# Second-part rows of a channel mixer split ahead of the first part's last down products, and its first two up tiles read from them

## The chip, the core and the metric

The kernel runs on one core of one Trainium2 chip. The time is device microseconds of one execution. Three runs of the kernel before are shown below; the profile and the trace are of a fourth execution of its own.

## What is computed

One inference step of a two-layer decoder trunk over 512 prompt rows and 32 sample rows, 1024 features wide. The reference, cut to what matters here:

```python
def swiglu(x, wg, wu, wd):
    return (jax.nn.silu(x @ wg) * (x @ wu)) @ wd          # D_FF = 2816
...
x = x + 0.5 * swiglu(rmsnorm(x, norm_ffa[i]), ffa_wg[i], ffa_wu[i], ffa_wd[i])
h = rmsnorm(x, norm_mix[i])
out = rwkv7_time_mix(h, ...) if i % 2 == 0 else mlstm_mix(h, ...)
x = x + out
x = x + 0.5 * swiglu(rmsnorm(x, norm_ffb[i]), ffb_wg[i], ffb_wu[i], ffb_wd[i])
```

The change is at the first channel mixer (`f0a`) and at the start of the RWKV mixer of layer 0.

## The kernel before

The 544 rows are held with features on the partitions, as eight tiles `x[k]` of 128x544, and are cut into two parts: rows 0 to 255 (`PARTS[0]`, 256 columns) and rows 256 to 543 (`PARTS[1]`, 288 columns). Every product is made of three TensorE instructions (`mm3`, L404 to L408) on operands split into a high and a low half; a weight tile of 128x1024 is loaded into one of three `wr` buffers, and each 512-wide half of it is rounded by ScalarE into `wh` (L401) and its remainder made by VectorE into `wl` (L402). There are four `wh` and four `wl` buffers, which is two weight tiles.

First `ffn` runs the whole mixer `f0a` for the first part: `norm_split` allots eight tiles `ts` of 128x2x544 (tag `a2`, ten buffers) and fills the high and low halves of `x * gain` into the columns of the first part alone (`split_scaled`, L454 on ScalarE and L455 on VectorE); the columns of the second part stay unused. Then come 22 up tiles (a `_g` and a `_u` product each, 24 matmuls a product) and eight down tiles (66 matmuls each, L493), each ending in an update of `x[m]` (L496). These use the pool `ffn` and eight PSUM banks `ps`.

Then the pools of `ffn` are closed and `rwkv` begins. The second part's rows of the same mixer are cut into units by `ffn_units` and used as filler between the steps of the RWKV mixer of the first part. `start` allots sixteen tiles `rk` in the new pool, fills them with the split rows, and takes the squares and the factor of the norm, `1/sqrt(mean(x^2)+eps)`, by one matmul pair with ones (L437), an Ln and an Exp. `up(m)` makes the `_g` and `_u` products into the two PSUM banks `pd`, multiplies both by the factor (L540, L541) and makes the sigmoid by Exp, Ln and Exp on ScalarE with three GpSimd operations in between; the result is split into `hm`. `down` adds to `x`. A list `todo` holds the units; `self.step(n)` issues the next n; `FILL` says how many after each step of `first`. The order of issue before is:

```python
self.rwkv_setup()                       # constants; ends with keep_table
first, second = self.rwkv_first(0)      # first[0] is rwkv_norm(0), first[1] mixes rows for w1, ...
self.todo = self.ffn_units(*before, 1, (0, 4, 8, 12, 16, 19, FT))
self.step()                             # start
for q, f in enumerate(first):
    f()
    self.step(FILL.get(q, 0))           # FILL[0] = 4: up0, up1, up2, up3 after rwkv_norm
```

`rwkv_norm(0)` (L697) takes the squares and the factor of the first part's new rows (again a matmul pair L437 into `pd`), multiplies the rows by it (L709) and forms the differences of neighbouring rows (L728, L730). `rwkv_mix` then makes from them the operands `mx` (L744 to L746) of the RWKV projections.

The instructions are not run in that order as it stands: when the kernel is built, a scheduler sets a fixed order for each engine. Of the instructions that are ready it takes the one issued first, so the order of issue is an order of rank; an instruction whose operands and buffers are ready early may be placed long ahead of its place in the program. On the chip each engine then keeps its fixed order and waits on semaphores.

Of the kernel before, what the change touches and what calls it, by code (L numbers as in the profile page):

```python
# [17 lines left out]
P = 128  # L18
D = 1024
KT = 8  # L20
FT = 22
# [5 lines left out]
HA = TP // 2  # L27
HB = TT - HA
# [7 lines left out]
NX = 4  # L36
WW = 512
NW = 4
FILL = {0: 4, 1: 4, 2: 1, 3: 4, 5: 3, 14: 3}
FILL2 = {5: 3, 6: 3, 9: 4}  # L40
PARTS = (slice(0, HA), slice(HA, TT))
NPAIR = 8
# [247 lines left out]
class Trunk:  # L290
# [149 lines left out]
    def norm_split(self, g, parts=PARTS):  # L440

        ts = [self.a2(F32R) for _ in range(KT)]
        rs = [self.tile("rms", 2, [P, HB])[:, :hs.stop - hs.start] for hs in parts]
        for hs in parts:
            self.split_scaled(g, hs, [(t[:, 0, hs], t[:, 1, hs]) for t in ts])
        for i, hs in enumerate(parts):
            for k in range(KT):
                self.squares(k, hs, rs[i])
        return [(t[:, 0, :], t[:, 1, :]) for t in ts], rs
# [7 lines left out]
    def ffn(self, name, g, parts=PARTS):  # L457
        xs, rs = self.norm_split(g, parts)
        hs_ = []
        lo_, hi_ = parts[0].start, parts[-1].stop  # L460
        parts = [(hs, slice(hs.start - lo_, hs.stop - lo_), hs.stop - hs.start) for hs in parts]
        for m in range(FT):
            wg = self.weight(self.a[name + "_g"][m])
            wu = self.weight(self.a[name + "_u"][m])
            hh, hl = [self.local("h", 44, [P, TT], F32R)[:, :hi_ - lo_] for _ in range(2)]
            for i, (hs, ds, w_) in enumerate(parts):
                pg, pu = self.ps(), self.ps()
                for ps, wt in ((pg, wg), (pu, wu)):
                    for k in range(KT):
                        c = slice(k * P, (k + 1) * P)  # L470
                        self.mm3(ps[:, :w_], *wt(c), xs[k][0][:, hs], xs[k][1][:, hs], k == 0, k == KT - 1)
                if m == 0:
                    self.norm_factor(rs[i], self.ps())
                s, w = self.t1(w_), self.t1(w_)
                self.V.tensor_tensor(s, pg[:, :w_], rs[i], op=ALU.mult)
                self.V.tensor_tensor(w, pu[:, :w_], rs[i], op=ALU.mult)
                self.last = self.S.activation(s, s, AF.Silu)
                self.G.tensor_tensor(s, s, w, op=ALU.mult)  # L478
                self.split(hh[:, ds], hl[:, ds], s)
            hs_.append((hh, hl))  # L480
            if m == 1 and name == "f0a":
                self.load_x(1)
        kb = (0, 8, 16, FT)
        for m in range(KT):
            pss = [self.ps() for _ in parts]

            def rows(b):
                return self.weight(self.a[name + "_d"][m][:, kb[b] * P:kb[b + 1] * P])

            def part(b, i, w):  # L490
                hs, ds, w_ = parts[i]
                for k in range(kb[b], kb[b + 1]):
                    c = slice((k - kb[b]) * P, (k - kb[b] + 1) * P)  # L493
                    self.mm3(pss[i][:, :w_], *w(c), hs_[k][0][:, ds], hs_[k][1][:, ds], k == 0, k == FT - 1)
                if b == 2:
                    self.V.scalar_tensor_tensor(self.x[m][:, hs], pss[i][:, :w_], 0.5, self.x[m][:, hs], op0=ALU.mult, op1=ALU.add)  # L496
            if m < KT - 1:
                for b in range(3):
                    w = rows(b)
                    for i in range(len(parts)):  # L500
                        part(b, i, w)
            else:
                ws = [rows(b) for b in range(3)]
                for i in range(len(parts)):
                    for b in range(3):
                        part(b, i, ws[b])
# [4 lines left out]
    def ffn_units(self, name, g, i, groups=(0, 6, 11, 17, FT)):  # L511


        V, S, G = self.V, self.S, self.G
        hs = PARTS[i]
        w_ = hs.stop - hs.start
        xs = []
        rs = self.tile("rms", 2, [P, HB])[:, :w_]
        h = {}

        def start():
            for k in range(KT):
                early = i == 0 and k < NX
                xs.append([self.local("xs", 2 * NX, [P, HA], F32R) if early else self.rk(i, F32R) for _ in range(2)])
            self.split_scaled(g, hs, xs)
            for k in range(KT):
                self.squares(k, hs, rs)
            self.norm_factor(rs, self.bank("pd", 2), True)

        def up(m):  # L530
            ps = []

            def half(n):
                ps.append(self.bank("pd", 2)[:, :w_])
                self.part_dense(self.weight(self.a[name + n][m]), ps[-1], xs)

            def second():
                half("_u")
                s, w, e = self.t1(w_), self.t1(w_), self.t1(w_)
                V.tensor_tensor(s, ps[0], rs, op=ALU.mult)  # L540
                V.tensor_tensor(w, ps[1], rs, op=ALU.mult)  # L541
                self.sigmoid(e, s)
                G.tensor_tensor(s, s, w, op=ALU.mult)
                G.tensor_tensor(s, s, e, op=ALU.mult)
                h[m] = [self.hm(w_) for _ in range(2)]
                self.split(*h[m], s)
            return Unit((24, lambda: half("_g")), (24, second))

        def down(m, k0, k1):
            wt = self.weight(self.a[name + "_d"][m][:, k0 * P:k1 * P])  # L550
            ps = self.bank("pd", 2)
            self.part_dense(wt, ps[:, :w_], [h[k] for k in range(k0, k1)])
            V.scalar_tensor_tensor(self.x[m][:, hs], ps[:, :w_], 0.5, self.x[m][:, hs], op0=ALU.mult, op1=ALU.add)
        us = [start]
        for k0, k1 in zip(groups, groups[1:]):
            us += [up(m) for m in range(k0, k1)]
            us += [Unit((3 * (k1 - k0), lambda m=m, k0=k0, k1=k1: down(m, k0, k1))) for m in range(KT)]
        return us

    def dense_units(self, ap, xs, evac):  # L560
# [47 lines left out]
    def rwkv(self, before=None, after=None):  # L608


        with self.scope("rw", nps=1):
# [4 lines left out]
            with self.tc.tile_pool(name="spill", bufs=1, space=DRAM) as dp:  # L616
# [5 lines left out]
                self.nhm = {"mx": NMX, "hm": 8}  # L622
                self.low, self.lowp = {}, dp
                with self.scope("rw1", nps=0):
                    self.rwkv_setup()
                    first, second = self.rwkv_first(0)
                    self.todo = self.ffn_units(*before, 1, (0, 4, 8, 12, 16, 19, FT))
                    self.step()
                    for q, f in enumerate(first):
                        f()  # L630
                        self.step(FILL.get(q, 0))
                    with self.tc.high_priority(OFF):
                        self.all_of(self.rwkv_ahead(0))
                        self.begin("quad", self.rwkv_square(0))
                        self.all_of(self.rwkv_rows(0))
                        self.drain("quad")
                    for q, f in enumerate(second):
                        f()
                        self.step(FILL2.get(q, 0))
                    with self.tc.high_priority(OFF):  # L640
                        self.all_of(self.rwkv_value(0))
                        self.all_of(self.rwkv_ahead(1))
                    first, second = self.rwkv_first(1)
                    self.todo += first
                    self.rwkv_slots(0, 10)
                    self.todo += second + self.rwkv_out(0, 0, 4)
                    self.rwkv_slots(10, 17)
# [24 lines left out]
    def rwkv_setup(self):  # L672
# [15 lines left out]
        w = self.a2(F32R).rearrange("p a b -> p (a b)")  # L688
        self.hg3 = w[:96, :TT]
        self.lg = w[:, TT:TT + 2 * P], w[:, TT + 2 * P:TT + 3 * P]  # L690
        self.pre = None
        self.keep_table()

    def rk(self, i, dt=F32):
        return self.rp(f"rk{i}", 17, [P, PARTS[i].stop - PARTS[i].start], dt)
# [1068 lines left out]
```

## Time and profile before

| | us |
|---|---|
| runs before | 2484.68, 2488.0, 2490.43; median 2488.0 |
| profiled execution | 2485.8 |
| its span, first to last instruction | 2483.9 |
| mean granted TensorE clock, share of full | 0.98 |

The profiled execution is 1.9 us longer than its span. Times in the rows below are microseconds from the start of the span. PE is TensorE's matmuls, PEld its weight loads, DVE VectorE, ACT ScalarE, POOL GpSimd. In the groups, `x8` is the number of instructions, and behind the bar stand their busy time in us, the mean of one in ns, and the idle time of the engine just before them. In the timelines the idle time ahead of an instruction and what ended it stand in brackets. A clock of 1.00 is the level of 2.4 GHz and 0.50 that of 1.2 GHz; values in between are means over a stretch.

### The profile page before, as it was taken

How to read it: one execution, taken by the hardware profiler on the slowest of the kernel's cores; microseconds unless marked ns; L12 is line 12 of the kernel's file. 1: busy time of each engine (PE TensorE's matmuls, PEld its weight loads, DVE VectorE, ACT ScalarE, POOL GpSimd, SP SyncE). 2: the span in 40 equal slices, each digit the busy share in tenths (PEclk: the TensorE clock that was granted, in tenths of full speed). 3: DMA queues.
4: the chain of work that ended last, by engine and by line, in shares of the span. 5: the costliest groups of instructions: out<-in, count | busy, mean ns of one | idle time of the engine just before them, and what ended most of it. 6: DMA issues, size and time to landing. Idle time of an engine off the chain costs nothing.

```text
span 2483.9 us, 54258 instructions
## 1 busy us (share of the span) xinstructions
PE 2404.3 (97%) x21731; PEld 2291.6 (92%) x21731; DVE 1562.1 (63%) x3202; ACT 1253.5 (50%) x2732; POOL 442.4 (18%) x458
## 2 busy tenths in 40 slices
PE   9998999998899999999999999999999999999997
PEld 8998988987788888898999999999978999999997
DVE  6667787788767888766666544443438766444333
ACT  6555666556676656565555433332345545333322
POOL 1202222333121244321110011110000000111100
PEclk9999999999899999999999999999999999999998
DMA  7564766434464343544555432322323323222232
GB/s 220 186 192 140 233 207 192 125 114 121 134 201 154 118 128 93 151 144 134 162 169 159 123 93 88 92 82 86 90 84 112 86 83 98 86 86 86 90 89 71
DMA packets 118348, 316.81 MB, mean 128 GB/s; under 512 B 14360, under 2 KB 30136, under 8 KB 118096
## 3 DMA queue, kind: packets, MB, share of 16 engines
q1 hardware_dynamic: 118096, 313.35, 41.3%
q8 instruction: 170, 2.79, 0.5%
q14 instruction: 82, 0.67, 0.1%
HBM read 291.34 MB, written 21.96 MB: 126 GB/s over the span
## 4 chain that ended last, share of the span: by engine, by line
PE 60%; DVE 2%; ACT 1%; DMA 1%; issue 0%; SPq 0%; DVEq 0%; POOL 0%; ACTq 0%
PE ps L406 15%; PE ps L408 15%; PE ps L407 15%; PE pd L406 3%; PE pd L407 3%; PE pd L408 2%; PE pc L284 1%; PE ps L284 1%; PE ps L1420 1%; PE ps L1422 1%; PE ps L1421 1%; DMA d<-dc 1%; PE b L284 0%; PE ps L281 0%; DVE wl L402 0%
## 5 line engine op out<-in xcount | busy, mean ns | idle before, releaser
L402 DVE TENSOR_TENSOR wl<-wr,wh 128x512 fp32r<-128x512 f32 (+2 forms) x993 | 692.6, 700 | 450.5 <-ACT wh L401 422.7
L401 ACT CAST wh<-wr 128x512 fp32r<-128x512 f32 (+2 forms) x993 | 593.3, 602 | 625.4 <-PE ps L407 431.6
L406 PE MATMUL ps<-a,wh 128*128 128x288 f32 (+1 forms) x2384 | 697.4, 293 | 13.2 <-DVE raw L1516 5.3
L408 PE MATMUL ps<-a,wl 128*128 128x288 f32 (+1 forms) x2384 | 692.4, 290 | 0.0
L407 PE MATMUL ps<-a,wh 128*128 128x288 f32 (+1 forms) x2384 | 686.7, 288 | 0.3
L406 PEld LDWEIGHTS ps<-a,wh 128*128 128x128 f32 x2384 | 452.6, 190 | 16.2 <-ACT a L454 5.5
L407 PEld LDWEIGHTS ps<-a,wh 128*128 128x128 f32 x2384 | 452.2, 190 | 1.6 <-DVE a L455 1.1
L408 PEld LDWEIGHTS ps<-a,wl 128*128 128x128 f32 x2384 | 449.9, 189 | 0.5 <-DVE wl L402 0.2
L406 PE MATMUL ps<-h,wh 128*128 128x288 f32 (+1 forms) x1056 | 303.9, 288 | 0.0
L407 PE MATMUL ps<-h,wh 128*128 128x288 f32 (+1 forms) x1056 | 303.4, 287 | 0.0
L408 PE MATMUL ps<-h,wl 128*128 128x288 f32 (+1 forms) x1056 | 303.2, 287 | 0.0
L478 POOL TENSOR_TENSOR t<-t,t 128x256 f32<-128x256 f32 (+1 forms) x132 | 141.7, 1074 | 856.7 <-ACT wh L401 409.5
L406 PE MATMUL pd<-rk,wh 128*128 128x288 f32 (+1 forms) x656 | 197.1, 301 | 6.2 <-ACT mx L745 3.7
L408 PEld LDWEIGHTS ps<-h,wl 128*128 128x128 f32 x1056 | 198.9, 188 | 0.0
L407 PEld LDWEIGHTS ps<-h,wh 128*128 128x128 f32 x1056 | 198.9, 188 | 0.0
L406 PEld LDWEIGHTS ps<-h,wh 128*128 128x128 f32 x1056 | 198.6, 188 | 0.0
L407 PE MATMUL pd<-rk,wh 128*128 128x288 f32 (+1 forms) x656 | 194.9, 297 | 0.0
L408 PE MATMUL pd<-rk,wl 128*128 128x288 f32 (+1 forms) x656 | 193.0, 294 | 0.0
L401 ACT CAST h<-t 128x256 fp32r<-128x256 f32 (+1 forms) x132 | 55.3, 419 | 199.2 <-POOL t L478 199.2
L406 PE MATMUL pd<-mx,wh 128*128 128x256 f32 (+1 forms) x448 | 133.1, 300 | 3.3 <-ACT mx L745 2.1
L406 PEld LDWEIGHTS pd<-rk,wh 128*128 128x128 f32 x656 | 125.7, 192 | 10.8 <-ACT mx L745 3.9
L407 PE MATMUL pd<-mx,wh 128*128 128x256 f32 (+1 forms) x448 | 132.9, 298 | 2.7 <-DVE mx L746 2.5
(516 smaller groups left out, 4537.5 us busy)
## 6 DMA issues: line engine op xcount, KB each, us to landing
wr<-in_f0a_u_dram SPq DMA_DIRECT2D x44, 512.0 KB, 3.9
wr<-in_f0b_g_dram SPq DMA_DIRECT2D x44, 512.0 KB, 3.6
wr<-in_f0b_u_dram SPq DMA_DIRECT2D x44, 512.0 KB, 3.6
wr<-in_f0a_g_dram SPq DMA_DIRECT2D x43, 512.0 KB, 3.6
wr<-in_f1a_g_dram SPq DMA_DIRECT2D x22, 512.0 KB, 4.2
wr<-in_f1a_u_dram SPq DMA_DIRECT2D x22, 512.0 KB, 3.5
wr<-in_f1b_g_dram SPq DMA_DIRECT2D x22, 512.0 KB, 3.5
wr<-in_f1b_u_dram SPq DMA_DIRECT2D x22, 512.0 KB, 3.5
```

What stands on the lines that cost most here:

```text
L284: r = f(*a, **k)
L401: self.S.copy(dst_h, src)
L402: self.V.tensor_tensor(dst_l, src, dst_h, op=ALU.subtract)
L406: T.matmul(out, wh, xh, start=start, stop=False)
L407: T.matmul(out, wh, xl, start=False, stop=False)
L408: T.matmul(out, wl, xh, start=False, stop=stop)
L478: self.G.tensor_tensor(s, s, w, op=ALU.mult)
L1420: T.matmul(pss[q][:n, :], xs[k][0][:, ts], wt(cs)[0], start=k == 0, stop=False)
L1421: T.matmul(pss[q][:n, :], xs[k][0][:, ts], wt(cs)[1], start=False, stop=False)
L1422: T.matmul(pss[q][:n, :], xs[k][1][:, ts], wt(cs)[0], start=False, stop=k == KT - 1)
```

## The change

- In `ffn`, for `f0a` and ahead of its third down tile (m = 2), the rows of the second part are split into the unused columns of `ts`, their squares are taken, and their factor is made into a tile `rs1`, by a Sqrt and a VectorE reciprocal in place of Ln and Exp.
- `ffn_units` for the second part uses `rs1`. Its first two up tiles read the split rows from `ts` and not from `rk`. `start` splits the rows into `rk` as before, but without squares and factor, and is now issued third, behind up0 and up1.
- In `rwkv`, up0, up1 and `start` are issued ahead of `rwkv_setup` and `rwkv_norm`; up2 and up3 follow behind `rwkv_norm` (FILL[0] is 2 in place of 4). `keep_table`, which loads ScalarE's table for Ln and Exp, moves from the end of `rwkv_setup` to ahead of up0.

```diff
-FILL = {0: 4, 1: 4, 2: 1, 3: 4, 5: 3, 14: 3}
+FILL = {0: 2, 1: 4, 2: 1, 3: 4, 5: 3, 14: 3}
...
     def norm_split(self, g, parts=PARTS):
         ts = [self.a2(F32R) for _ in range(KT)]
+        self.ts = ts
...
         for m in range(KT):
+            if name == "f0a" and m == 2:
+                self.rs1 = self.tile("rms", 2, [P, HB])
+                self.split_scaled(g, PARTS[1], [(t[:, 0, HA:], t[:, 1, HA:]) for t in self.ts])
+                for k in range(KT):
+                    self.squares(k, PARTS[1], self.rs1)
+                self.norm_factor(self.rs1, self.ps())
             pss = [self.ps() for _ in parts]
...
-        rs = self.tile("rms", 2, [P, HB])[:, :w_]
+        ready = [(t[:, 0, hs], t[:, 1, hs]) for t in self.ts] if i else None
+        rs = self.rs1 if i else self.tile("rms", 2, [P, HB])[:, :w_]
...
             self.split_scaled(g, hs, xs)
-            for k in range(KT):
-                self.squares(k, hs, rs)
-            self.norm_factor(rs, self.bank("pd", 2), True)
+            if not i:
+                for k in range(KT):
+                    self.squares(k, hs, rs)
+                self.norm_factor(rs, self.bank("pd", 2), True)
...
-                self.part_dense(self.weight(self.a[name + n][m]), ps[-1], xs)
+                self.part_dense(self.weight(self.a[name + n][m]), ps[-1], ready if ready and m < 2 else xs)
...
+        if ready:
+            us[:3] = us[1], us[2], us[0]
...
                 with self.scope("rw1", nps=0):
+                    self.todo = self.ffn_units(*before, 1, (0, 4, 8, 12, 16, 19, FT))
+                    self.keep_table()
+                    self.step(3)
                     self.rwkv_setup()
                     first, second = self.rwkv_first(0)
-                    self.todo = self.ffn_units(*before, 1, (0, 4, 8, 12, 16, 19, FT))
-                    self.step()
...
-        self.pre = None
-        self.keep_table()
```

## Rows read from the trace of the kernel before

**Rows 1.** The page's first line: span and number of instructions.

```profile
span 2483.9 us, 54258 instructions
```

**Rows 2.** Stretches: length, each engine's busy time (instructions), clock, DMA share, GB/s.

```profile
140.00:199.50 59.50, 59.50 (x507) 59.40 (x505) 35.66 (x66) 30.83 (x58) 0.00 (x0) 1.00 0.69 199
199.50:203.60 4.10, 1.19 (x5) 0.60 (x5) 3.42 (x11) 4.08 (x10) 0.00 (x0) 1.00 0.88 280
203.60:207.00 3.40, 3.40 (x16) 3.37 (x15) 3.36 (x10) 3.17 (x10) 0.00 (x0) 0.54 0.83 293
...
211.80:215.50 3.70, 0.04 (x1) 0.00 (x0) 3.70 (x13) 2.02 (x6) 0.00 (x0) 0.82 0.15 19
215.50:221.00 5.50, 5.42 (x23) 5.45 (x24) 5.29 (x11) 2.55 (x8) 4.33 (x3) 0.50 0.51 178
221.00:239.90 18.90, 18.90 (x141) 18.51 (x140) 16.45 (x33) 12.38 (x27) 8.12 (x8) 1.00 0.41 119
...
242.30:247.10 4.80, 4.51 (x30) 4.08 (x31) 3.67 (x7) 1.76 (x3) 0.00 (x0) 1.00 0.10 19
...
350.00:353.40 3.40, 0.85 (x8) 0.65 (x7) 3.40 (x7) 2.25 (x4) 1.56 (x2) 1.00 0.44 165
353.40:358.00 4.60, 4.27 (x33) 3.93 (x33) 4.60 (x6) 1.42 (x3) 3.73 (x3) 0.63 0.20 61
```

**Rows 3.** TensorE's timeline from the last down product to the first low-rank product: start, us, instruction, idle before.

```profile
199.32 0.28 PE L408 MATMUL ps<-h,wl 128*128 128x256 f32 x1
201.25 0.75 PE L437 MATMUL pd<-rms,c_c_all 128*128 128x288 f32 x2 [1.65 <-DVE x L496]
203.27 0.70 PE L437 MATMUL pd<-rms,c_c_all 128*128 128x256 f32 x2 [1.26 <-DVE rms L424]
203.62 0.55 PE L406 MATMUL pd<-rk,wh 128*128 128x288 f32 x1
...
215.58 0.58 PE L406 MATMUL pd<-rk,wh 128*128 128x288 f32 x1 [3.74 <-ACT mx L745]
...
242.27 0.53 PE L406 MATMUL pd<-hm,wh 128*128 128x288 f32 x2 [2.35 <-ACT hm L401]
...
247.13 0.28 PE L406 MATMUL pd<-mx,wh 128*128 128x256 f32 x1
```

**Rows 4.** VectorE's timeline at the same place, cut.

```profile
205.41 2.85 DVE L709 SCALAR_TENSOR_TENSOR x<-x,c_vecs,rms 128x256 f32<-128x256 f32 x7
...
212.60 1.28 DVE L402 TENSOR_TENSOR wl<-wr,wh 128x512 fp32r<-128x512 f32 x2
...
214.99 0.45 DVE L540 TENSOR_TENSOR t<-pd,rms 128x288 f32<-128x288 f32 x1
```

**Rows 5.** Groups of VectorE and ScalarE, 199.5 to 242.3 us.

```profile
L454 ACT ACTIVATE rk<-x,c_vecs 128x288 fp32r<-128x288 f32 x8 | 4.0, 525 | 0.0
L455 DVE SCALAR_TENSOR_TENSOR rk<-x,c_vecs,rk 128x288 fp32r<-128x288 f32 x8 | 3.8, 510 | 0.0
L709 DVE SCALAR_TENSOR_TENSOR x<-x,c_vecs,rms 128x256 f32<-128x256 f32 x8 | 3.3, 478 | 0.0
L728 DVE TENSOR_TENSOR gm<-x 128x255 f32<-128x255 f32 x8 | 3.2, 410 | 0.0
```

**Rows 6.** Timelines and a group: what the moved norm factor is made of.

```profile
135.54 1.28 ACT L829 ACT_TABLE_LOAD   x1
17.71 1.75 DVE L433 RECIPROCAL rms<-rms 128x256 f32<-128x256 f32 x1 [1.44 <-ACT rms L432]
L422 ACT ACTIVATE t<-x 128x288 f32<-128x288 f32 (+1 forms) x13 | 5.5, 432 | 2.5 <-DVE x L496 2.3 <-DVE h L402 0.2
```

**Rows 7.** Timelines of VectorE and GpSimd: one operation alone and beside GpSimd.

```profile
227.16 0.47 DVE L744 SCALAR_TENSOR_TENSOR m<-gm,c_vecs,x 128x256 f32<-128x256 f32 x1
228.16 1.03 DVE L744 SCALAR_TENSOR_TENSOR m<-gm,c_vecs,x 128x256 f32<-128x256 f32 x1
...
227.75 1.17 POOL L543 TENSOR_TENSOR t<-t,t 128x288 f32<-128x288 f32 x1
```

## The prediction

> **What bounds the kernel now.** I read four views. The page gives the span [rows 1], and the profiled execution took 2485.8 us, 1.9 us more. The table of stretches then says where TensorE isn't at work or isn't at full clock around the change [rows 2]: through the down products of the first part (140 to 199.5 us) it is busy 59.50 of 59.50 us at clock 1.00, so nothing else limits it there. Then, at the seam to the RWKV mixer, it is busy 1.19 of 4.10 us, works 3.4 us at clock 0.54, stands still for 3.7 us, and works 5.42 us at clock 0.50. From 221 us on it is full again at 1.00. TensorE's timeline names the waits [rows 3]: 1.65 us behind the last update of x, 1.26 us for the squares of the first part's new rows, 3.74 us ahead of up1, and 2.35 us ahead of the first down products that need up3. VectorE's timeline shows what TensorE waited for at 215.58 [rows 4]. The row names ScalarE, but the bank of up0's first product comes free by L540, which starts at 214.99, so that is what ended the wait. L540 stood behind the norm of the first part (L709), the last of the row splits, the weight splits of 212.60 and more: VectorE is busy 3.70 of 3.70 us there. The seam is thus bound by VectorE's queue and by the order of rank in it, and each idle stretch of 3 to 4 us was followed by the lower clock level of 1.2 GHz.
>
> **The change part by part.**
>
> *Work taken ahead of the seam.* Eight splits on ScalarE at 0.525 us and eight on VectorE at 0.510 [rows 5] are added, 4.2 and 4.1 us, since `start` still makes its own. Their operands are there early and they use no pool that opens late, so the scheduler may place them anywhere in the idle time of `f0a`. In the down stretch alone VectorE has 59.50 - 35.66 = 23.8 us free and ScalarE 28.7 [rows 2]. The squares ran among the down products before, too (they are part of the group of L422) [rows 6]. A table load of 1.28 us for Sqrt comes on ScalarE, and a reciprocal on VectorE: 1.75 us for 256 columns, so about 2.0 for 288 [rows 6]. I cost all of this at nothing. What hides it is that two weight tiles are kept ready, four halves, each lasting TensorE about 1.4 us (12 of 507 matmuls of 59.50 us [rows 2]). An operation of 2 us in front of a weight split fits in there; if that cover is gone, the bound is the reciprocal and the table load, 3.3 us. What isn't hidden is the matmul pair of the norm factor, which now stands between down products on a full TensorE: at most the 0.75 us that it took at the seam [rows 3], at least half of that at full clock; I take 0.5.
>
> *Start of up0.* It needs neither the pair nor the splits of `start` any more, but still a bank of the new pool, which before was had only behind L496, at 201.25 [rows 3]. So up0 starts there and not at 203.62: 2.37 us gained (none if another wait stays; 4.0 if the bank comes at once).
>
> *Clock after the seam.* The idle time in front falls to 1.65 us, with a full stream behind it. The nearest row is the wait of 2.35 us ahead of 242.27, after which the clock stayed at 1.00 [rows 2, 3]. So 3.40 us at 0.54 no longer cost 3.40 x 0.46 = 1.6 us (none gained, if it falls all the same).
>
> *Wait of up1.* up0 and up1 now rank above `start` and `rwkv_norm`, so L540 no longer stands behind L709: 3.74 us gained, and the half clock behind it, 5.42 x 0.50 = 2.7 us [rows 2, 3]. Together the seam gives 2.4 + 1.6 + 3.7 + 2.7 = 10.4 us.
>
> *What is late next.* `rwkv_norm`. Its matmul pair needs one of two `pd` banks, and up0 and up1 hold both by rank. Before, it ran at 203.27; now it comes behind up1. Four products at 24 x 18.90/141 = 3.2 us [rows 2] from 201.25 + 0.5 end at 214.6. There the pair costs 0.4 and the handing over of a bank about as much, 0.75 us in all (0.4 to 1.1). up2 runs from 215.3 to 221.7; its splits `rk`, 3.8 us of VectorE [rows 5], have all of up0 and up1 to be made in. L709 started 2.1 us after the pair before (203.27 to 205.41) [rows 3, 4], so now at 216.7, and with L709 and the differences, 3.3 and 3.2 us plus eight one-column operations, VectorE is taken up for some 6.9 us to 223.6 [rows 5]. These rank above up2's L540, which frees the bank of up3, and above up3's weight splits. With an L540 of 0.45 and half a weight tile (0.64) behind them [rows 4], less what overlaps, up3 begins at 224.3 in place of 221.7: a new wait of 2.6 us. It lies between 0, if the scheduler finds room for the splits in between, and 5.8 us, if GpSimd's operations for up1 slow these operations (L744 took 1.03 us beside L543, and 0.47 alone [rows 7]; three GpSimd operations of 1.17 us for an up tile would add 1.9) and a whole weight tile comes behind.
>
> On this the Trainium skill, page "SBUF — State Buffer", section "Who interferes with whom", has a rule that speaks against the change: a VectorE instruction with two SBUF inputs and a GpSimd instruction that reads SBUF exclude each other for the whole of one. The two L744 rows agree [rows 7]. By it the norm, which met no GpSimd work before, now meets that of up1, which puts the wait near 4.6 us and the gain near 2; by the undisturbed rows it is 2.6 and 4.8.
>
> *Clock after the new wait.* 2.35 us of idling was followed by 1.00, but 2.55 us of it (in 350 to 353.4) by 4.60 us at 0.63, 1.7 us lost [rows 2, 3]. 2.6 us is nearer to the second: I take 1.7 (0 to 2.7).
>
> *What stays.* The wait ahead of the first down products is the time of up3's chain through ScalarE and GpSimd less what TensorE has in hand, both unchanged: 2.35 us again. Behind it TensorE is nearly full, so what is gained by then should reach the end.
>
> Sum: 10.4 - 0.5 - 0.75 - 2.6 - 1.7 = 4.85, say 4.8 us. Against the profiled execution that is 2485.8 - 4.8 = 2481.0; the median of the runs is 2.2 higher, so 2488.0 - 4.8 = 2483.2 us.
>
> **The rivals.**
>
> *VectorE keeps up.* No new wait at up3 and no clock loss there: 10.4 - 1.25 = 9.15 us, 2478.9. For it: in 221 to 239.9 VectorE has 2.4 us free [rows 2]. Against it: none of its work has left the seam except the order of it, and 203.6 to 221 was without a gap.
>
> *The wait only moves.* The upper bounds hold, 5.8 us at up3 and 2.7 for the clock: 10.4 - 1.25 - 8.5 = 0.65 us gained, 2487.4; the same if a later stretch that is bound by VectorE, as 350 to 358 (busy 8.00 of 8.00 us [rows 2]), takes the gain back. For it: the L744 rows, and the rule named above, which is a case of this one. Against it: TensorE's lead is carried by all that runs behind it.
>
> *Slower: the norm of the first part comes too late.* If its pair gets a bank only behind up3, at about 227.5, then L709, the differences and eight mixes (0.47 us each alone, 1.03 beside GpSimd [rows 7], and 0.47 for the low half) fill VectorE for 14 to 19 us, and with six weight halves at 0.64 between them the first low-rank product waits until 247 to 250, where it began before at 247.1 [rows 3]. TensorE has the eight products and four down tiles by 237 and idles some 10 us, then starts at half clock (2.7 us); the second mix, queued behind, is later by the same. That is 2 to 9 us lost, around 2494. It decides from the point where the pair slips by more than about 20 us against 203.27. Against it: the pair ranks above up2, so a bank that up1 gives back should go to it.
>
> **How the numbers follow.** A measurement of this kernel can tell about 0.2%, 5.0 us, from no change. Forecast (a shorter wait at up3, gain 2.5 to 8.5 us; own range 2479.5 to 2485.5): 0.58, with a little under half above 5.0 us. VectorE keeps up: 0.16. The wait only moves, or the gain is given back (gain -2 to 2.5): 0.17. Slower: 0.09. So faster is 0.27 + 0.16 = 0.43, within 0.2% 0.31 + 0.17 = 0.48, slower 0.09. The range reaches down to a full gain with the bank had at once (2488.0 - 9.15 - 1.65 = 2477.2) and up to the far end of the third case, 2490.0; the slower case and a strip of the best are left out.
>
> **What would show it.** Right, if the profile of the changed kernel shows: up0's first matmul on tile `a` in place of `rk` at about 201.8 behind L496; a clock of 1.00 from there to about 214, with no wait over 1 us; both 96 matmuls and then the 256-column pair L437; the next wait of 2 to 6 us at up2 or up3 with L709 or L728 in front of L540 on VectorE; and the matmul of 242.27 at about 237.5. The down products stay gapless from 140 to 199.5 but for the pair. Wrong, if the 256-column pair still runs ahead of up0, if splits stand in front of weight splits during `f0a` and TensorE waits there, if the half clock still follows the seam, or if the lead at 237.5 is gone further on.

## The result and the profile after

The changed kernel took 2503.35 us (median of 4 runs, 2501.36 to 2504.78), beside 2488.6 us for the kernel before on the same chip: a ratio of 1.0059, 95% interval 1.0046 to 1.0071. It is slower by 14.7 us; forecast were 2483.2 us and a range from 2477.2 to 2490.0. Measured once more on another chip it took 2502.75 us beside 2491.15, 1.0048 (1.0036 to 1.0060).

The page's first line after, against [rows 1]:

```profile
span 2501.5 us, 54280 instructions
```

The table of stretches after, with the columns of [rows 2]:

```profile
140.00:200.00 60.00, 60.00 (x510) 59.89 (x509) 36.90 (x63) 32.90 (x58) 1.28 (x1) 1.00 0.67 196
200.00:218.20 18.20, 17.16 (x133) 16.77 (x131) 13.36 (x29) 12.01 (x25) 2.90 (x3) 1.00 0.69 211
218.20:226.30 8.10, 0.03 (x2) 0.01 (x1) 4.97 (x11) 4.61 (x12) 2.66 (x3) 0.82 0.36 99
226.30:229.50 3.20, 3.20 (x12) 3.02 (x13) 0.99 (x3) 1.16 (x4) 0.00 (x0) 0.50 0.00 0
229.50:235.00 5.50, 5.50 (x40) 5.41 (x39) 5.50 (x21) 2.83 (x10) 0.00 (x0) 0.94 0.00 0
...
247.00:250.60 3.60, 0.24 (x2) 0.02 (x1) 3.16 (x6) 1.74 (x5) 2.71 (x3) 1.00 0.45 139
250.60:256.00 5.40, 4.88 (x19) 4.51 (x20) 4.25 (x10) 2.04 (x6) 0.00 (x0) 0.51 0.04 7
256.00:260.00 4.00, 4.00 (x28) 4.00 (x28) 2.63 (x6) 2.05 (x5) 0.00 (x0) 0.81 0.43 124
```

The down products are full, as before. Then 18 us look as forecast, at clock 1.00. From 218.2 on TensorE stands still for 8.1 us, and *no* engine is full in that time: VectorE is busy 4.97 of 8.10 us, ScalarE 4.61. So no engine's throughput is the limit there; a chain is, that is, instructions on several engines of which each waits for the one before. Half clock follows that wait and the next one.

TensorE's timeline after at the seam, against [rows 3] (from 205.29 to 218.2 the 96 matmuls of up0 and up1 follow without a gap):

```profile
205.29 0.37 PE L406 MATMUL pd<-a,wh 128*128 128x288 f32 x1 [1.04 <-DVE der L694]
226.29 1.22 PE L437 MATMUL pd<-rms,c_c_all 128*128 128x256 f32 x2 [8.07 <-DVE rms L424]
236.04 0.37 PE L406 MATMUL pd<-rk,wh 128*128 128x288 f32 x1 [0.89 <-DVE t L551]
...
250.62 0.82 PE L406 MATMUL pd<-hm,wh 128*128 128x288 f32 x2 [3.38 <-ACT hm L401]
```

The wait of 8.07 us stands at the 256-column pair, which makes the norm factor of the *first* part, and it is ended by the sum of squares (L424). ScalarE's timeline shows when those squares were taken:

```profile
150.27 0.42 ACT L422 ACTIVATE rms<-x 128x256 f32<-128x256 f32 x1 [0.38 <-DVE x L504]
...
220.85 0.44 ACT L859 ACTIVATE t<-t 128x288 f32<-128x288 f32 x1
221.20 0.40 ACT L422 ACTIVATE t<-x 128x256 f32<-128x256 f32 x1
222.54 0.42 ACT L422 ACTIVATE t<-x 128x256 f32<-128x256 f32 x1 [0.94 <-DVE rms L424]
222.86 0.41 ACT L401 CAST hm<-t 128x288 fp32r<-128x288 f32 x1
223.19 1.92 ACT L422 ACTIVATE t<-x 128x256 f32<-128x256 f32 x5
```

Only the first square (k = 0), which goes straight into `rms`, runs among the down products, at 150.27, as soon as its row tile is ready. The other seven go into a tile `t`, and all seven stand behind the last Exp of up1 (220.85). In the kernel before six of the seven ran among the down products (the first and the last of the six follow), and the seventh at 201.23:

```profile
153.89 0.42 ACT L422 ACTIVATE t<-x 128x256 f32<-128x256 f32 x1 [0.39 <-DVE x L496]
...
192.76 0.42 ACT L422 ACTIVATE t<-x 128x256 f32<-128x256 f32 x1 [0.38 <-DVE x L496]
```

GpSimd's timeline has up1's product of its two halves just ahead of them:

```profile
220.33 0.79 POOL L554 TENSOR_TENSOR t<-t,t 128x288 f32<-128x288 f32 x1
```

It ends at 221.12, and the first of the seven squares starts at 221.20. The code, cut, says why this could be:

```python
NT1 = 3
def t1(self, w=HB):   return self.tile("t1", NT1, [P, HB])[:, :w]
# squares(): sq = acc if k == 0 else self.t1(...)
# up(m):     s, w, e = self.t1(w_), self.t1(w_), self.t1(w_)
```

The squares and the up tiles' temporaries share three buffers, and whoever is issued first gets them first. Before, the squares of `rwkv_norm(0)` were issued ahead of every up tile. Now up0 and up1 are issued first and take a buffer six times, and up1's three come free only as its chain through ScalarE and GpSimd ends.

Where the time goes over the whole run is read by matmul count: the time at which a kernel starts its n-th matmul, less the time at which the kernel before starts its n-th (a median over 8 to 20 us around the time named). This difference is called the lag. Where a kernel runs its matmuls in another order, work done earlier or later counts in it too.

| lag, us, at (time of before) | 34 | 178 | 271 | 425 | 661 | 919 | span |
|---|---|---|---|---|---|---|---|
| after | 4.2 | 4.4 | 11.1 | 13.3 | 8.0 | 17.6 | 17.6 |
| after, second profile | 3.9 | 4.2 | 10.8 | 13.8 | 9.2 | 17.8 | 19.6 |

So about 4 us arise at the very start, 6.7 at the seam, and the rest, 6.5 us net (8.8 in the second profile), behind 271. The start is read in TensorE's timeline:

```profile
13.47 0.58 PE L406 MATMUL ps<-a,wh 128*128 128x256 f32 x1 [0.52 <-ACT wh L401]
26.65 0.39 PE L408 MATMUL ps<-a,wl 128*128 128x256 f32 x1 [0.96 <-DVE wl L402]
```

and in ScalarE's:

```profile
17.05 0.53 ACT L455 ACTIVATE a<-x,c_vecs 128x288 fp32r<-128x288 f32 x1
...
20.03 1.38 ACT L455 ACTIVATE a<-x,c_vecs 128x288 fp32r<-128x288 f32 x3
21.82 1.39 ACT L455 ACTIVATE a<-x,c_vecs 128x288 fp32r<-128x288 f32 x3
```

The early splits were placed not among the down products but at 17 to 26 us, where the first weight tiles are still being made, and the wait at 26.65 is behind them. The wait at 13.47 lies ahead of all of them: the rounding of that weight on ScalarE, at 12.80, stood 1.11 us behind a DMA, where in the kernel before it started at 11.69. Behind this wait TensorE's 128x256 matmuls go on starting every 0.21 us until 18.4 and only then every 0.12 us; in the kernel before the faster pace begins by 13.3. The trace's record of the granted clock begins only with that step (at 18.6 us, and at 12.8 in the kernel before); ahead of it the clock column of a table of stretches reads 1.00, so the pace shows this and not the column. Over all profiles (the experiments below included) it comes at 17.3 to 18.6 us where TensorE waited 0.3 to 0.9 us near 13.5 us (after twice, e6, e7, e11), and at 13.3 to 14.4 us in all others. The eight splits don't decide that: e2, e4 and e8 have all eight early, no such wait, and a lag of 2.5 to 2.8 us at 34 us; e11 has one split early, and the wait. What moves the landing isn't shown. Of the 4 us at the start, an estimate from these lags gives about 1.5 us to this wait and not quite 2 us to the splits, which is what the kernels without the wait lose by having them early.

### The profile page after: what moved, and what is told of

It is laid out like the page before. It is cut to its first block, busy times and chain, and to the rows that moved or that the text cites. A ratio compares the mean times of both kernels' runs of the same rounds, so it can differ in the third digit from the quotient of the medians.

```text
span 2501.5 us, 54280 instructions
## 1 busy us (share of the span) xinstructions
PE 2408.5 (96%) x21731; PEld 2295.2 (92%) x21731; DVE 1567.5 (63%) x3211; ACT 1255.6 (50%) x2740; POOL 445.5 (18%) x458
## 4 chain that ended last, share of the span: by engine, by line
PE 83%; DVE 9%; DMA 3%; ACT 3%; issue 2%; POOL 1%; SPq 0%; DVEq 0%; ACTq 0%; POOLq 0%
PE ps L406 18%; PE ps L408 17%; PE ps L407 17%; PE pd L406 7%; PE pd L407 6%; PE pd L408 6%; PE pc L284 2%; DVE wl L402 2%; PE b L284 1%; PE ps L284 1%; DVE m L756 1%; PE pq L284 1%; PE ps L1432 1%; PE ps L1434 1%; PE ps L1433 1%
## 5 line engine op out<-in xcount | busy, mean ns | idle before, releaser
L406 PE MATMUL pd<-rk,wh 128*128 128x288 f32 (+1 forms) x624 | 188.5, 303 | 5.0 <-ACT rk L401 2.3
L407 PE MATMUL pd<-rk,wh 128*128 128x288 f32 (+1 forms) x624 | 184.8, 296 | 0.0
L408 PE MATMUL pd<-rk,wl 128*128 128x288 f32 (+1 forms) x624 | 184.4, 296 | 0.0
L477 DVE TENSOR_TENSOR t<-ps,rms 128x256 f32<-128x256 f32 (+1 forms) x132 | 58.1, 440 | 122.3 <-PE ps L408 121.7
```

What stands on the lines that cost most here:

```text
L406: T.matmul(out, wh, xh, start=start, stop=False)
L407: T.matmul(out, wh, xl, start=False, stop=False)
L408: T.matmul(out, wl, xh, start=False, stop=stop)
```

## The experiments

Every kernel below was timed beside the kernel before on the same chip, in three rounds on three chips (medians of before 2491.06, 2491.06 and 2491.15 us). In the cuts of the edits, "..." stands for lines left out.

**Squares first (e2).** The first part's squares are issued ahead of up0; everything else is the changed kernel.

```diff
                     self.keep_table()
+                    self.rs0 = self.tile("rms", 2, [P, HB])[:, :HA]
+                    for k in range(KT):
+                        self.squares(k, PARTS[0], self.rs0)
                     self.step(3)
...
```

> The changed kernel, with the squares of the first part's norm issued ahead of up0 and up1, so that they get the t1 buffers first; nothing else moves. Theory 1: the squares run among the down products again, the 8.07 us wait and the half clock behind it go (TensorE's lag against the kernel before falls from 11 to 4 us or less at 280 us), 2490 to 2496 us. Rival A: 2500 or more. Rival B: the wait goes but the later stages lose as much as now, 2495 to 2499.

Measured 2491.62 us, ratio 1.0001 (0.9991 to 1.0011): the slowdown is gone. TensorE's timeline:

```profile
203.91 0.37 PE L406 MATMUL pd<-a,wh 128*128 128x288 f32 x1 [1.03 <-DVE der L697]
216.58 0.59 PE L437 MATMUL pd<-rms,c_c_all 128*128 128x256 f32 x2
217.38 0.37 PE L406 MATMUL pd<-rk,wh 128*128 128x288 f32 x1 [0.21 <-ACT wh L401]
225.59 0.37 PE L406 MATMUL pd<-rk,wh 128*128 128x288 f32 x1 [1.58 <-DVE t L551]
...
236.76 0.38 PE L406 MATMUL pd<-hm,wh 128*128 128x288 f32 x1 [2.08 <-DVE t L552]
239.14 0.85 PE L406 MATMUL pd<-hm,wh 128*128 128x288 f32 x2 [0.94 <-ACT hm L401]
241.39 0.61 PE L407 MATMUL pd<-hm,wh 128*128 128x288 f32 x1 [1.40 <-DVE hm L402]
```

The pair now follows up1 with no wait, and the lag, 3.0 us at 178, is 0.1 at 271. On ScalarE the squares stand among the down products again; the second of the seven:

```profile
164.94 0.42 ACT L422 ACTIVATE t<-x 128x256 f32<-128x256 f32 x1 [0.39 <-DVE x L504]
```

Beside the changed kernel the lag at 271 is 11.0 us less, and the median ends 0.6 us behind the kernel before in place of 14.7 and 11.6. So most of the slowdown goes with the buffers at the seam, although the changed kernel's lag grows behind 271 as well.

**Squares elsewhere (e7).** e2 moves the squares in rank and in buffers at once. Here the order of issue stays that of the changed kernel, and only the buffer differs: the squares go into columns of `ts` that are free by then, and are rounded to the type of that tile.

```diff
-        sq = acc if k == 0 else self.t1(hs.stop - hs.start)
+        sq = acc if k == 0 else self.ts[k][:, 0, hs] if spare else self.t1(hs.stop - hs.start)
...
-            self.squares(k, hs, rs)
+            self.squares(k, hs, rs, not i)      # in rwkv_norm
...
```

> The changed kernel with the same order of issue, but the squares of the first part's norm (k = 1 to 7) are written into columns of the first mixer's split tiles that are free by then, and not into the three t1 buffers (they are rounded to the tile's type; the sum is otherwise the same). Theory, that the squares waited for t1 buffers handed to up0 and up1 first: the squares run among the down products, the wait of 8 us falls under 1.5 us, and the time is that of the kernel with the squares issued first, 2490 to 2493. Rival, that they were late because they rank behind up1: the wait stays 5 us or more, 2500 to 2504.

Measured 2490.49 us, 1.0000 (0.9986 to 1.0013). TensorE's timeline, the pair again without a wait:

```profile
205.01 0.38 PE L406 MATMUL pd<-a,wh 128*128 128x288 f32 x1 [1.04 <-DVE der L694]
217.79 0.59 PE L437 MATMUL pd<-rms,c_c_all 128*128 128x256 f32 x2
```

and ScalarE's, where each square runs as its row tile gets ready:

```profile
160.51 0.42 ACT L422 ACTIVATE a<-x 128x256 fp32r<-128x256 f32 x1
166.04 0.42 ACT L422 ACTIVATE a<-x 128x256 fp32r<-128x256 f32 x1 [0.39 <-DVE x L504]
...
205.06 0.40 ACT L422 ACTIVATE a<-x 128x256 fp32r<-128x256 f32 x1
```

The rank behind up1 did not hold the squares back; the three buffers did. That settles the cause at the seam.

**Late splits (e1), and both (e3).** In e1 each early ScalarE split has an order edge on the last Silu of `f0a`; e3 is e1 and e2 together.

```diff
-            self.S.activation(hi, self.x[k][:, hs], AF.Identity, scale=gv)
+            r = self.S.activation(hi, self.x[k][:, hs], AF.Identity, scale=gv)
+            if last is not None:
+                self.after(r, last)
...
```

> The changed kernel, with the eight ScalarE splits of the second part's rows ordered behind the last Silu of f0a, so that none can stand among the weight splits of the start (17 to 26 us). Theory 1 (the squares of the first part's norm wait for the three t1 buffers, which go out in program order and so to up0 and up1 first; that is the 8.07 us wait of TensorE at 226 us): that wait stays at 7 to 9 us, the start gets back the about 2 us that TensorE lost from 18 to 34 us, so 2500 to 2502 us. Rival A (the early splits are the main loss, by delaying everything behind them): 2496 or less. Rival B (the order of the later RWKV stages is the main loss): 2501 to 2504.

> Both edits together (late splits, squares first). Theory 1: what I had forecast for the change as it was meant, a gain of 0 to 5 us over the kernel before, 2483 to 2489 us. Rival A: equal to the run with late splits alone. Rival B: still 5 us or more over the kernel before, 2494 or more, with the seam itself no longer behind.

e1: 2496.45 us, 1.0024 (1.0015 to 1.0034), between what its theory and rival A expected. The 8.07 us wait stays:

```profile
223.48 1.22 PE L437 MATMUL pd<-rms,c_c_all 128*128 128x256 f32 x2 [8.07 <-DVE rms L424]
```

The lag at 34 us is 0.9 in place of 4.2. From 178 to 271 it grows by 6.8, and then it grows no further. e3: 2498.64 us, 1.0030 (1.0014 to 1.0045), where the theory expected a gain: its seam is as good as that of e2 (lag 0.1 at 271), but it falls back by 9.3 us from 425 to 919. The two repairs don't add up.

**Old order (e4, e5).** The order of issue is that of the kernel before; of the change there stay the early splits, squares and factor, and up0 and up1 that read them (e4), with the splits held late as in e1 (e5).

```diff
-FILL = {0: 2, 1: 4, 2: 1, 3: 4, 5: 3, 14: 3}
+FILL = {0: 4, 1: 4, 2: 1, 3: 4, 5: 3, 14: 3}
...
-            us[:3] = us[1], us[2], us[0]
...
```

> One half of the change alone: the early splits, the early factor and up0 and up1 reading them, in the order of issue of the kernel before (setup, start, first part's norm, then up0 to up3). Theory 1: the squares keep the t1 buffers, so no 8 us wait; VectorE's queue ahead of up0's first multiplication stays, so little is gained: 2487 to 2492 us. Rival A: the start's loss alone, 2491 to 2493. Rival B (it is the new order of issue that costs, by way of the later stages): 2486 to 2490.

> The changed kernel, but the split units, the norm and the up tiles are issued in the old order, and ScalarE's early splits wait for the last Silu. What stays of the change: the splits, squares and factor of the second part are made among the first down products. If the early splits' only price is the 2 us at the start, this is 2 us better than the kernel with the old order alone (2494.1), so about 2492, with the 4.3 us wait at the 256-column pair still there. Rival, that the early work costs something in the down stretch too: still 2494 or more.

e4: 2494.14 us, 1.0010 (1.0000 to 1.0019), slower than any of its expectations; TensorE waits 4.33 us at the pair, now ahead of up0:

```profile
206.97 1.19 PE L437 MATMUL pd<-rms,c_c_all 128*128 128x256 f32 x2 [4.33 <-DVE rms L424]
```

e5: 2495.29 us, 1.0017 (1.0007 to 1.0027), no better than e4, though its start lag is 0.7 in place of 2.5. The theory that the splits' 2 us at the start reach the end fell here.

**One split late (e6), and the changed kernel again (e9).** e6 is e1 with the edge on the last split (k = 7) alone. Its seam is that of the changed kernel, but the fixed order of VectorE's instructions from about 600 us on is again nearer to that of before. In the traces, 135 of VectorE's 2324 instructions there stand out of the order of before in the changed kernel, and 7 in e6.

> The changed kernel with one added order: the last of the eight early ScalarE splits waits for the last Silu, the seven others stay. Start and seam are those of the changed kernel (the 8 us wait at the 256-column pair stays), but on VectorE the order of work behind 640 us is again that of the kernel before. Theory, that about 6 us of the changed kernel's 14.7 come from the other order in the later RWKV stages: 2496 to 2499, no growth of the lag behind 640 us. Rival, that the later growth follows from the late seam itself: 2503, as the changed kernel.

> The changed kernel itself, beside the next two and the kernel before on one chip. If the order of work in the later stages is worth about 5 us, this stays behind the kernel in which one split was held late (2498.7): 2502 to 2505. If not: 2497 to 2500.

e6: 2498.67 us, 1.0032 (1.0020 to 1.0045); e9, the changed kernel, 2502.75. The medians stand 4.1 us apart as the order theory wanted, but the intervals of the two ratios overlap. In the profiles the lag of e6 grows by 0.1 us from 425 to 919 and that of the changed kernel by 4.3 and 4.0. But e6 loses more ahead of that (6.0 us from 271 to 425, beside 2.2 and 3.0), so that at 919 us the three stand nearly alike (16.2, 17.6, 17.8). So e6 bears the theory out by its median and by the growth, and not by where its profile ends; that profile is of one of its slowest executions (2502.13).

**One unit more (e8, e11), and the same unit without the change (e10).** e8 is e2 with a down product more behind up3; this keeps the later order nearer to that of before (7 instructions out of it). e11 is e8 with seven of the eight splits held late. e10 is the kernel *before* with that unit.

```diff
-FILL = {0: 2, 1: 4, 2: 1, 3: 4, 5: 3, 14: 3}
+FILL = {0: 3, 1: 4, 2: 1, 3: 4, 5: 3, 14: 3}      # e8, e11; in e10 {0: 5, ...} for {0: 4, ...}
```

> The kernel with the squares issued first (2491.6), and one unit more in the first slot of the low-rank products. With it VectorE's order of work from some 900 us on is again that of the kernel before. Theory, that the later order costs about 5 us there: 2486 to 2489, under the kernel before. Rival, that the lag of that kernel at 900 us came from elsewhere: 2491 to 2493.

> The kernel before with one unit more in the first slot of the low-rank products (a first down product behind up3), and nothing of the change. Theory, that the 4.6 us by which the changed kernel with early squares and this unit beat the kernel before come from the earlier up tiles at the seam: no gain here, 2489 to 2492. Rival, that they come from the unit alone: 2485 to 2488.

> The changed kernel with the first part's squares issued first, one unit more in the first slot, and seven of the eight early ScalarE splits held behind the last Silu; the later order of work stays that of the kernel before. If the early splits cost about 2 us at the start and nothing hides it later: 2484 to 2486, under 2486.5. If the start's delay does not reach the end: 2486 to 2489.

e8: 2486.49 us, 0.9986 (0.9977 to 0.9995), the best of all and faster than both kernels, by 4.6 us against the kernel before. e11: 2487.77, 0.9987 (0.9978 to 0.9997), so holding the splits late gives nothing more. e10: 2488.51, 0.9990 (0.9982 to 0.9999). That lies between the times that its two theories gave: 2.6 of e8's 4.6 us come from the unit alone, which has nothing to do with the change. What the change itself gives in e8 is then about 2 us and within the error.

The lags of these kernels, as in the table above, and how many of the 2324 VectorE instructions behind 600 us stand out of the order of before (135 in the changed kernel):

| | 34 | 178 | 271 | 425 | 661 | 919 | span | out of order |
|---|---|---|---|---|---|---|---|---|
| e1 | 0.9 | 1.8 | 8.6 | 9.1 | 6.1 | 8.2 | 7.8 | 5 |
| e2 | 2.8 | 3.0 | 0.1 | 0.7 | -2.5 | 6.5 | 4.1 | 231 |
| e3 | 1.0 | 2.2 | 0.1 | 1.7 | -3.1 | 11.0 | 10.2 | 142 |
| e4 | 2.5 | 2.8 | 3.5 | 4.4 | 4.2 | 7.0 | 8.8 | 14 |
| e5 | 0.7 | 1.9 | 3.8 | 8.8 | 8.2 | 12.6 | 12.7 | 71 |
| e6 | 3.4 | 3.6 | 10.1 | 16.1 | 13.8 | 16.2 | 16.4 | 7 |
| e7 | 3.9 | 4.1 | 2.3 | 6.0 | -1.3 | 6.4 | 4.2 | 301 |
| e8 | 2.5 | 2.8 | 0.0 | 1.4 | -0.1 | 1.7 | -0.6 | 7 |
| e10 | 0.6 | 0.6 | 2.8 | 2.9 | -0.3 | 2.0 | 2.2 | 7 |
| e11 | 2.8 | 3.6 | 1.0 | 4.0 | 3.3 | 5.3 | 6.2 | 14 |

From 425 to 919 the kernels with 135 and more out of order (after twice, e2, e3, e7) fall back by 0.4 to 9.3 us, those with 14 and fewer change by -0.9 to 2.6. (e5 has 71, and its 3.8 us stand between.) The two groups overlap by one kernel: e7, with the most out of order, falls back by 0.4 alone.

## Why the prediction was wrong

**What bounds the kernel** was read rightly as far as it went: the waits of [rows 3] and the queue of VectorE. What it didn't read is who holds `t1`.

**Start of up0, clock, wait of up1**: right. up0 starts right behind the last update of x on VectorE, which ends at 205.15 (L694 in its row is a short operation behind that), with 1.04 us of idling in front (1.65 forecast), at clock 1.00, and up1 follows without a wait. The two waits of 1.26 and 3.74 us and the half clock at 203.6 and 215.5 [rows 2, 3] are gone.

**Work taken ahead**: the squares (142 to 147 us), the Sqrt with its table load (1.28 us) and the reciprocal (1.95 us, forecast about 2.0) are hidden, and the pair costs little among full down products. "I cost all of this at nothing" fails for the splits: the scheduler put them at 17 to 26 us, where two weight tiles in hand were not yet there. The lag at 34 us is 2.5 to 4.2 in the kernels with all eight splits early (after, e2, e4, e7, e8), 0.7 to 1.0 with all late (e1, e3, e5). Not all of it is theirs: e11, with one split early, has 2.8, behind a weight that landed late. And the end doesn't show it (e4 beside e5, e8 beside e11).

**What is late next: the step that failed.** "Its matmul pair needs one of two `pd` banks", with 0.75 us put down for it, named the right operation and the wrong resource. The sentence "The squares ran among the down products before, too" was true of before and was carried over silently, though the change issues six takers of `t1` ahead of those squares. In place of 0.75 us the pair waited 8.07 us, with 1.9 us lost to the half clock behind it (0.50 from 226.3 to about 230.2), and L721, which is L709 of the kernel before and was forecast for 216.7, started at 228.51. The later waits go with it: the wait for `hm` grows from 2.35 to 3.38 us, and 5.40 us at 0.51 follow. e1 and e6, which keep the 8 us wait, have 3.37 and 3.38 us there; in e2 and e7 no wait up to there is over 2.1 us. From 205 to 260 us TensorE's seven waits of 0.5 us and more sum to 15.2 us, and the four stretches under full clock (3.20 us at 0.50, 5.50 at 0.94, 5.40 at 0.51, 4.00 at 0.81) lose 5.3 us; before it was 9.0 us in four waits [rows 3] and 4.3 us in two stretches [rows 2]. That is 7.2 us worse, less the 288-column pair of 0.75 us that left the seam; the lag grew by 6.7 us (4.4 to 11.1). Freed of the buffers (e2, e7) the same seam gains 2.9 and 1.8 us instead.

**The slower rival** had the right sign and the right victim, and its mark, a pair more than 20 us later than 203.27, was passed (226.29, 23.0 later). Its mechanism, a bank given back only behind up3, did not occur, its loss of 2 to 9 us was 14.7, and the chance of 0.09 was too low: a norm that the change puts behind two units should have been followed through *every* buffer it takes.

**The new wait at up3** is seen where the squares are not late: 1.58 us in e2 (2.6 forecast). The clock stays at 1.00 behind it, so the 1.7 us put down for the clock there were not lost. "What stays" failed there: the first down products wait 2.08, 0.94 and 1.40 us in e2, not 2.35, and the clock is at 0.50 from 238.6 to 245.4. VectorE is the reason in e2:

```profile
220.00:240.00 20.00, 14.83 (x99) 13.20 (x97) 20.00 (x48) 11.25 (x30) 7.83 (x7) 0.97 0.27 82
240.00:260.00 20.00, 18.22 (x122) 17.50 (x123) 19.54 (x48) 12.04 (x27) 2.08 (x1) 0.86 0.49 146
```

It is busy 20.00 of 20.00 us, with 7.83 us of GpSimd beside it. VectorE's timeline of the changed kernel shows the price of that company: two L758 took 1.97 us while L554 and L555 ran on GpSimd (238.96 to 241.03), the next one, alone, 0.41:

```profile
236.41 1.44 DVE L756 SCALAR_TENSOR_TENSOR m<-gm,c_vecs,x 128x256 f32<-128x256 f32 x3
...
239.34 1.97 DVE L758 TENSOR_TENSOR mx<-m,mx 128x256 fp32r<-128x256 f32 x2
...
241.83 0.41 DVE L758 TENSOR_TENSOR mx<-m,mx 128x256 fp32r<-128x256 f32 x1
```

The rule of the Trainium skill that the prediction weighed (page "SBUF — State Buffer", section "Who interferes with whom") says that a VectorE instruction with two inputs in SBUF and a GpSimd instruction that reads SBUF exclude each other; the two L758 agree. Not every row does: beside L848, a GpSimd operation with one input in SBUF (236.46 to 237.68), the three L756 took 0.48 us each, as alone. The L744 of [rows 7] that took 0.47 us, called alone there, ran beside such an operation too (L836, 226.00 to 227.67). The rule bears on the seam of e2, not on the wait that decided here, in which VectorE was free for 3 of 8 us.

**"What is gained by then should reach the end"** did not hold in every kernel. In e2 the 2.9 us gained at the seam only made good the 3.0 us lost ahead of it: it stood 0.1 us behind the kernel before at 271 us, and its median ended 0.6 us behind. e3 stood there as well, and its median ended 7.6 us behind. The later order of instructions, which the scheduler fixes anew for every edit, may be the cause: between 425 and 919 us the means of the two groups above differ by about 4 us. But the groups overlap, and that order was never changed alone, so this is argued and not shown. Open stay the few us by which kernels with nearly the same later order differ between 271 and 425 us (e6 +6.0, e1 +0.5), and why e3 ends so far behind.

## What to carry to other kernels

When work is issued ahead of other work, list every pool that both draw from, temporaries as well as PSUM banks, and follow who gets which buffer in the order of issue; a small ring of temporaries that two chains share makes the second wait for the end of the first. A stretch in which TensorE idles and no other engine is full is the mark of such a chain: look which instruction is the first behind the gap and which buffer it writes. And in a kernel whose order is fixed by a scheduler, an edit of a few us at one place is measured together with a reordering elsewhere, which may be worth as much: run a neutral edit as well, before a gain or a loss is put down to the change.

## What was not expected of the hardware

What the half clock cost did not follow the length of the wait. In the wait of 8.07 us the granted clock fell to 0.50 at 223.4, while TensorE still stood idle, and rose at 230.2, so that only the 3.9 us of work behind the wait met it. At the wait of 3.38 us it fell at 250.7, just as the work began, and rose at 257.5, so that nearly all of those 6.8 us were work. The shorter wait cost more.
